# Seven block products for eight in the up projection of a two-layer trunk: what it does on one Trainium2 core

## The chip, the core and the metric

The kernel runs on one core of a Trainium2 chip. The metric is the time of one execution on the device, in microseconds (us); lower is better. The core has a matrix engine (TensorE, PE), VectorE (DVE), ScalarE (ACT), GpSimd (POOL) and SyncE (SP), which issues the DMAs here. The engines run side by side and wait for one another through semaphores.

## The reference

One step of a two-layer trunk over 576 tokens: 64 new tokens of 8 sequences and a prompt of 512. Each layer has a token mixing (attention and two linear recurrences), then a ConvFFN; the change is in the ConvFFN. With D = 1024, D_FF = 2816 and `L` tokens of a sequence:

```python
xn = rms_norm(x, p['g_pre_ffn'])
u = xn @ p['w_up']                                   # (1024) x (1024 x 5632)
ext = jnp.concatenate([conv_prev.astype(u.dtype), u], axis=1)
c = sum(ext[:, j:j + L] * p['w_conv'][j] for j in range(CONV_WIDTH))   # width 3
a, b = jnp.split(c, 2, axis=-1)
ffn = (jax.nn.gelu(a, approximate=True) * b) @ p['w_down']             # (2816 x 1024)
x = x + rms_norm(ffn, p['g_post_ffn'])
```

## The kernel before, in words

Activations lie transposed: features on the 128 partitions (eight k-tiles of the model width, `KT`), the 576 tokens along the free axis, in two halves of 320 and 256 (`HALVES`). Every f32 product is made from two parts of each operand: a high part (a rounded copy) and the low rest. Three matmuls, high x high, high x low, low x high, go into one PSUM bank (`gemm`, L121 to L127).

A weight tile is 128 x 1024. `load_w` (L110) loads it by SP into a raw buffer of a ring of three (`wraw`); `split_w` (L103) has ACT copy the high part `whi` (L106) and DVE subtract for the low part `wlo` (L107).

`ffn` is the loop of interest. The up projection has 44 column tiles a layer, in 22 pairs: tile 2j gives the gelu side of 128 hidden columns, 2j+1 the other. Per up tile (`col_tile`), half 0 is `col_half` (8 x 3 matmuls of 320), half 1 is `joint_half`: `wh` goes against high and low tokens side by side (512 wide, L151), `wl` against the high ones (256 wide, L150 and L153), and ACT's copy (L156) and a DVE add (L157) join the two sums. The first three tiles of a layer are made in `first_tiles`, k-tile by k-tile, as the normed activations come. The evacuation multiplies by the norm's factor `R` into `u` (L1065, L1067, L1069), `conv_end` makes the width-3 convolution (ACT L1083, DVE L1084 and L1085, and two small POOL copies of state, L1076 and L1077), and after the second tile of a pair `h_tile` makes gelu (ACT L1095), the product (DVE L1096) and its split into high and low parts (ACT L1111, DVE L1115).

The down projection is spread over three groups of hidden tiles, and the last five go through `final_phase`, which also makes the closing norm:

```python
FF_GROUPS = ((0, 6), (6, 6), (12, 5))
```

All eight down tiles of a group stand together, behind the up pair after the group's last one (loop at L1143 to L1160). A down tile loads its weights, makes both halves and adds the result to `y` (ACT L1134 in the first group, DVE L1136 and L1139).

On every engine the instructions stand in one order, fixed when the program is built: a scheduler takes them from the order of the code and its costs, `behind(...)` and `manual_schedule` set the rest by hand. An engine that waits holds all that stands behind in its order.

Of the kernel before, what the change touches and what calls it, by code (L numbers as in the profile page):

```python
# [72 lines left out]
def trunk_kernel(ctx: ExitStack, tc: tile.TileContext, I, O):  # L73
# [68 lines left out]
    def joint_half(w, xh, xm, ks, evac, add=None):  # L142


        t0, n = HALVES[1]
        b = main_bank()
        for i, k in enumerate(ks):
            wh, wl = wtile(w, i)
            if i:
                PE.matmul(b[:, :n], wl, xh[k][1], start=False, stop=False)  # L150
            PE.matmul(b[:, :2 * n], wh, xm[k], start=(i == 0), stop=(i == len(ks) - 1))  # L151
            if i == 0:
                PE.matmul(b[:, :n], wl, xh[k][1], start=False, stop=False)  # L153
        if add is None:
            low = columns(n, "low", 2)
            S.activation(low, b[:, n:2 * n], AF.Copy)  # L156
            V.tensor_tensor(b[:, :n], b[:, :n], low, ALU.add)  # L157
        evac(b, 1, t0, n)
        if add is not None:
            add(b[:, n:2 * n], t0, n)  # L160

    def col_tile(w, xh, xl, ks, evac, name=None, xm=None, add=None):
        for hf in range(2):
            with behind(placed.get(FILL.get(f"{name}:{hf}"))):
                if hf and xm is not None:
                    joint_half(w, xh, xm, ks, evac, add)
                else:
                    col_half(w, xh, xl, ks, hf, evac)
# [1203 lines left out]
```

## Time and profile before

| | |
|---|---|
| median of 3 runs | 1708.03 us (1703.61 to 1710.71) |
| profiled execution | 1708.13 us, span of its trace 1706.3 us |
| mean granted TensorE clock | 0.989 |

The span runs from the first to the last instruction of the trace; the execution's own time is 1.8 us longer. Rows of groups give line, engine, operation, output <- inputs, tile size and count, then busy time and mean ns of one, and the idle time before them with what ended it. In a timeline, the first number is the start in us from the span's start, the second how long it took; "x3" means that three are shown as one, and a bracket tells an idle time before and its releaser. Layer 0's up tiles begin at 447 us.

### The profile page before, as it was taken

What the parts mean: (1) busy time and instruction counts of PE and PEld (TensorE: products, weight loads), DVE (VectorE), ACT (ScalarE), POOL (GpSimd) and SP (SyncE); (2) the same over time, 40 slices, a digit from 0 to 9 for tenths busy, and PEclk for the clock granted to TensorE, in tenths of its full rate; (3) what the DMA queues carried; (4) which work ended last, traced back from release to release, by engine and by line L of the source; (5) the groups of instructions that cost most, each with busy time, mean ns of one, the idle gap of its engine ahead of it and who ended that gap; (6) DMA issues with size and microseconds to landing.
All of it is one profiled execution on the core that took longest, in us unless ns stands there. A gap on an engine that the chain in (4) does not pass through costs nothing.

```text
span 1706.3 us, 34557 instructions
## 1 busy us (share of the span) xinstructions
PE 1655.1 (97%) x13840; PEld 1541.0 (90%) x13840; DVE 1118.3 (66%) x2270; ACT 780.4 (46%) x1376; POOL 525.6 (31%) x800
## 2 busy tenths in 40 slices
PE   8999999999999999999989999989999999999997
PEld 8888997789899999999988899968998999999997
DVE  6765756557774674776657657566578737757764
ACT  6744425574543442443456544255645434324431
POOL 4554332304420220230365453332053202103203
PEclk9999999999999999999999999999999999999999
DMA  5221336846344535633222212378555355266231
GB/s 184 70 70 58 103 116 241 335 169 258 136 148 161 198 107 215 230 120 112 97 79 83 76 64 79 120 299 312 186 201 185 109 195 206 73 234 255 70 105 56
DMA packets 65664, 260.83 MB, mean 153 GB/s; under 512 B 9664, under 2 KB 18144, under 8 KB 63968
## 3 DMA queue, kind: packets, MB, share of 16 engines
q1 hardware_dynamic: 65504, 258.62, 43.1%
q8 instruction: 109, 1.79, 0.4%
q14 instruction: 51, 0.42, 0.1%
HBM read 245.39 MB, written 80.31 MB: 191 GB/s over the span
## 4 chain that ended last, share of the span: by engine, by line
PE 86%; ACT 4%; POOL 3%; DVE 3%; issue 2%; DMA 1%; SPq 0%; POOLq 0%; ACTq 0%; DVEq 0%
PE ps_m L125 18%; PE ps_m L127 18%; PE ps_m L126 18%; PE ps_m L151 12%; PE ps_m L150 5%; PE ps_s L511 2%; PE ps_o L983 1%; PE ps_o L887 1%; PE ps_s L897 1%; POOL x L370 1%; PE ps_m L663 1%; PE ps_t L916 1%; PE ps_m L153 1%; PE ps_m L421 1%; PE ps_s L949 1%
## 5 line engine op out<-in xcount | busy, mean ns | idle before, releaser
L125 PE MATMUL ps_m<-xha,whi 128*128 128x320 f32 x1088 | 342.2, 315 | 3.1 <-ACT whi L106 2.6
L126 PE MATMUL ps_m<-xla,whi 128*128 128x320 f32 x1088 | 341.3, 314 | 0.0
L127 PE MATMUL ps_m<-xha,wlo 128*128 128x320 f32 x1088 | 340.2, 314 | 0.9 <-DVE wlo L107 0.9
L107 DVE TENSOR_TENSOR wlo<-wraw,whi 128x1024 fp32r<-128x1024 f32 (+4 forms) x232 | 259.0, 1121 | 77.2 <-ACT whi L106 74.9
L106 ACT ACTIVATE whi<-wraw 128x1024 fp32r<-128x1024 f32 (+4 forms) x232 | 221.1, 959 | 169.4 <-PE ps_m L126 64.7
L151 PE MATMUL ps_m<-xm,whi 128*128 128x512 f32 x656 | 237.6, 396 | 0.0
L126 PEld LDWEIGHTS ps_m<-xla,whi 128*128 128x128 f32 x1088 | 207.0, 190 | 5.8 <-issue 2.0
L125 PEld LDWEIGHTS ps_m<-xha,whi 128*128 128x128 f32 x1088 | 207.2, 190 | 5.5 <-ACT whi L106 2.8
L127 PEld LDWEIGHTS ps_m<-xha,wlo 128*128 128x128 f32 x1088 | 206.7, 190 | 3.1 <-issue 1.4
L150 PE MATMUL ps_m<-xm,wlo 128*128 128x256 f32 x574 | 161.2, 281 | 0.0
L125 PE MATMUL ps_m<-hh,whi 128*128 128x320 f32 (+1 forms) x512 | 154.1, 301 | 0.0
L126 PE MATMUL ps_m<-hh,whi 128*128 128x320 f32 (+1 forms) x512 | 154.1, 301 | 0.0
L127 PE MATMUL ps_m<-hh,wlo 128*128 128x320 f32 (+1 forms) x512 | 154.0, 301 | 0.0
L1077 POOL COPY cso<-u 128x2 f32<-128x2 f32 x88 | 79.2, 900 | 209.9 <-DVE u L1069 209.4
L151 PEld LDWEIGHTS ps_m<-xm,whi 128*128 128x128 f32 x656 | 123.3, 188 | 22.4
L127 PE MATMUL ps_m<-xm,wlo 128*128 128x256 f32 x432 | 124.6, 288 | 0.0
L125 PE MATMUL ps_m<-xm,whi 128*128 128x256 f32 x432 | 124.5, 288 | 0.0
L126 PE MATMUL ps_m<-xm,whi 128*128 128x256 f32 x432 | 123.5, 286 | 0.0
L150 PEld LDWEIGHTS ps_m<-xm,wlo 128*128 128x128 f32 x574 | 108.6, 189 | 3.4
L126 PEld LDWEIGHTS ps_m<-hh,whi 128*128 128x128 f32 x512 | 96.5, 188 | 1.5
L125 PEld LDWEIGHTS ps_m<-hh,whi 128*128 128x128 f32 x512 | 96.5, 189 | 0.3 <-DVE y L400 0.3
L127 PEld LDWEIGHTS ps_m<-hh,wlo 128*128 128x128 f32 x512 | 96.7, 189 | 0.0
(326 smaller groups left out, 3843.6 us busy)
## 6 DMA issues: line engine op xcount, KB each, us to landing
wraw<-in_w_up SPq DMA_DIRECT2D x88, 512.0 KB, 3.6
kv<-in_ck SPq DMA_DIRECT2D x32, 768.0 KB, 6.9
kv<-in_cv SPq DMA_DIRECT2D x32, 768.0 KB, 6.9
out_ck<-in_ck SPq DMA_DIRECT2D x32, 768.0 KB, 7.5
out_cv<-in_cv SPq DMA_DIRECT2D x32, 768.0 KB, 6.7
wraw<-in_w_s SPq DMA_DIRECT2D x42, 512.0 KB, 3.7
wraw<-in_w_dn SPq DMA_DIRECT2D x32, 384.0 KB, 3.1
wraw<-in_w_v SPq DMA_DIRECT2D x12, 512.0 KB, 3.6
```

Source lines behind the costliest of these rows:

```text
L106: S.activation(hi[:, :n], raw[:, :n], AF.Copy)
L107: V.tensor_tensor(lo[:, :n], raw[:, :n], hi[:, :n].bitcast(F32), ALU.subtract)
L125: PE.matmul(out, ah, bh, start=(i == 0), stop=False)
L126: PE.matmul(out, ah, bl, start=False, stop=False)
L127: PE.matmul(out, al, bh, start=False, stop=(i == n - 1))
L150: PE.matmul(b[:, :n], wl, xh[k][1], start=False, stop=False)
L151: PE.matmul(b[:, :2 * n], wh, xm[k], start=(i == 0), stop=(i == len(ks) - 1))
L153: PE.matmul(b[:, :n], wl, xh[k][1], start=False, stop=False)
L370: (V if dram_out and k % 4 == 3 else G).tensor_tensor(xk, xk, yk, ALU.add)
L421: PE.matmul(b[:, :n], wh, xh, start=(k == 0), stop=False)
L511: mm = PE.matmul(bp[64 * hh:64 * hh + 64, cp * nh * 32:(cp + 1) * nh * 32], xk[:, c0:c0 + 64], moving(c0), start=True, stop=True)
L1077: G.tensor_copy(cso[:, ui, 16:18], u[:, NU - 2:NU])
```

## The change

Pairs 4 to 21 of each layer ("fast pairs") are made by Strassen's scheme: the 1024 model features are taken as two halves, the pair's two column tiles as two, the 576 tokens as two halves of 288. Eight block products become seven (`products`), each of 4 k-tiles x 3 matmuls x 288 columns, that add up in three banks; ACT keeps copies of partial sums (`keep`), and VectorE or ACT evacuates the sums into `u`.

Both operands need sums of blocks. For the tokens `combine` makes them once a layer, in four parts behind up tiles 3 to 6: it scales by the gain and `R` first (so the fast evacuation has no factor), builds sums in `y` (not yet in use) and splits seven blocks into high and low parts. For the weights `weights` makes four block adds of 512 columns on DVE for each pair and splits 3 x 1024 + 512 columns, instead of 2 x 1024.

Pairs 0 to 3 stay plain, with the joint half replaced by 8 x 3 matmuls of 256 there and in all down tiles. The down tiles form four groups and stand one, two or four at a time behind single pairs (`FF_AFTER`). The convolution's `c` has two buffers instead of three, and hidden tiles 2 to 9 of the ring of ten lie where the activations lay. `x` is written out to DRAM at the end of each mixing (16 stores of half a tile) and read back (8 loads) before `final_phase`, since its place is used for the new weight tiles.

```diff
-FF_GROUPS = ((0, 6), (6, 6), (12, 5))
+FF_GROUPS = ((0, 4), (4, 4), (8, 4), (12, 5))
+FF_AFTER = ({4: 2, 5: 2, 6: 2, 7: 2}, {8: 2, 9: 2, 10: 2, 11: 2}, {12: 2, 13: 2, 14: 2, 15: 2},
+            {17: 1, 18: 1, 19: 1, 20: 1, 22: 4})
...
+            def combine(i):
+                with behind(last_lo[0].ins):
+                    x1, x2, ua, ta = (y[4 * (i % 2) + m] for m in range(4))
+                    for k, d in ((i, x1), (i + HK, x2)):
+                        V.scalar_tensor_tensor(d, xt[k], gnorm(l, 2, k), R, ALU.mult, ALU.mult)
+                    V.tensor_tensor(ua[:, :SH], x1[:, :SH], x1[:, SH:], ALU.subtract)
+                    V.scalar_tensor_tensor(ua[:, SH:], x2[:, SH:], -1.0, ua[:, :SH], ALU.mult, ALU.subtract)
+                    V.tensor_tensor(ta[:, :SH], x2[:, SH:], x1[:, SH:], ALU.subtract)
+                    V.scalar_tensor_tensor(ta[:, SH:], ua[:, SH:], -1.0, x2[:, :SH], ALU.mult, ALU.subtract)
+                    hi, lo = (cp.tile([P, 7 * SH], F32R, name=f"{n}{i}", tag=f"{n}{i}") for n in ("sxh", "sxl"))
+                    for src, m, n in ((x1[:, :SH], B11, 1), (x2, B21, 2), (ua, U1, 2), (ta, T3, 2)):
+                        cols = slice(m * SH, (m + n) * SH)
+                        S.activation(hi[:, cols], src, AF.Copy)
+                        V.tensor_tensor(lo[:, cols], src, hi[:, cols].bitcast(F32), ALU.subtract)
...
+            def weights(j):
+                r0, r1 = (wp.tile([P, WN], F32, name="wraw", tag="wraw", bufs=3) for _ in range(2))
...
+                w0 = split_w(r0, WN, sw, 2)
+                V.tensor_tensor(ws[:, b], r0[:, a], r1[:, a], ALU.add)
+                V.tensor_tensor(r1[:, a], r1[:, a], r1[:, b], ALU.add)
+                V.tensor_tensor(ws[:, a], r0[:, a], r1[:, a], ALU.add)
+                w2 = split_w(ws, WN)
+                w1 = split_w(r1, WN, sw, 2)
+                V.tensor_tensor(r0[:, b], r0[:, b], ws[:, a], ALU.add)
+                w3 = split_w(r0[:, b], HW)
...
+                product(ba, w0, 0, B11)
+                p1 = keep(ba)
+                product(bb, w0, 1, B21)
+                e1(0, lambda d, c: V.tensor_tensor(d, c(bb), c(p1), ALU.add))
+                product(ba, w2, 0, U2, True)
+                p16 = keep(ba)
+                product(bc, w1, 0, U1)
+                p5 = keep(bc)
+                product(ba, w2, 1, T3, True)
+                e2(1, lambda d, c: V.scalar_tensor_tensor(d, c(ba), -1.0, c(p5), ALU.mult, ALU.subtract))
+                product(bc, w3, 0, B22, True)
+                e1(1, lambda d, c: V.tensor_tensor(d, c(bc), c(p16), ALU.add), True)
+                product(ba, w1, 1, T4, True)
+                e2(0, lambda d, c: S.activation(d, c(ba), AF.Copy, scale=-1.0), True)
```

Three places of the program's order show what moves. In each row stands the line, the operation, output <- inputs with buffer numbers, and the size. The first place is VectorE around the evacuation of up tile 6 of layer 0 (`u_5907`; `u_5970` is tile 7's), before:

```order
L1069 TENSOR_TENSOR u_5907<-ps_m_5937,rbc_5168 128x256
L1115 TENSOR_TENSOR hh_5894<-c_5888,hh_5894 128x64
L1115 TENSOR_TENSOR hh_5894<-c_5888,hh_5894 128x2x256
L1065 TENSOR_TENSOR u_5970<-ps_m_5973,rbc_5168 128x8x8
L1067 TENSOR_TENSOR u_5970<-ps_m_5973,rbc_5168 128x256
L1084 SCALAR_TENSOR_TENSOR c_5960<-u_5907,par_90,c_5960 128x592
L1085 SCALAR_TENSOR_TENSOR c_5960<-u_5907,par_90,c_5960 128x592
L157 TENSOR_TENSOR ps_m_6000<-ps_m_6000,low_6017 128x256
L1069 TENSOR_TENSOR u_5970<-ps_m_6000,rbc_5168 128x256
L107 TENSOR_TENSOR wlo_6174<-wraw_6171,whi_6173 128x1024
```

and with the change (tile 6's is `u_5998`; `wlo_6167`, `wlo_6178` and `wlo_6174` are low parts of pair 4's weights, `sxl2` and the rows of L1119 and L1121 are `combine`):

```order
L114 TENSOR_TENSOR wlo_6167<-wraw_6161,whi_6166 128x1024
L1119 SCALAR_TENSOR_TENSOR y6_4689<-y5_4688,y6_4689 128x288
L1121 SCALAR_TENSOR_TENSOR y3_4686<-y2_4685,y1_4684 128x288
L114 TENSOR_TENSOR wlo_6178<-wraw_6162,whi_6177 128x1024
L1126 TENSOR_TENSOR sxl2_5981<-y2_4685,sxh2_5980 128x576
L1077 SCALAR_TENSOR_TENSOR c_5778<-u_5720,par_90,c_5778 128x592
L114 TENSOR_TENSOR wlo_6174<-ws_6165,whi_6173 128x1024
L1055 TENSOR_TENSOR u_5998<-ps_m_6001,rbc_5168 128x8x8
L1055 TENSOR_TENSOR u_5998<-ps_m_6001,rbc_5168 128x256
L1055 TENSOR_TENSOR u_5998<-ps_m_6028,rbc_5168 128x256
L1143 TENSOR_TENSOR wraw_6161<-wraw_6161,ws_6165 128x512
```

The ten rows before hold one weight split of 1024 columns among the evacuations; now three splits, of the next pair, and pieces of `combine` stand ahead of the tile's first evacuation.

The second place is VectorE in the up tiles, before (tiles 10 and 11 of layer 0):

```order
L1069 TENSOR_TENSOR u_6177<-ps_m_6207,rbc_5168 128x256
L107 TENSOR_TENSOR wlo_6372<-wraw_6369,whi_6371 128x1024
L1084 SCALAR_TENSOR_TENSOR c_6230<-u_6177,par_90,c_6230 128x592
L1065 TENSOR_TENSOR u_6240<-ps_m_6243,rbc_5168 128x8x8
L1067 TENSOR_TENSOR u_6240<-ps_m_6243,rbc_5168 128x256
L1085 SCALAR_TENSOR_TENSOR c_6230<-u_6177,par_90,c_6230 128x592
L157 TENSOR_TENSOR ps_m_6270<-ps_m_6270,low_6287 128x256
L1069 TENSOR_TENSOR u_6240<-ps_m_6270,rbc_5168 128x256
L107 TENSOR_TENSOR wlo_6444<-wraw_6441,whi_6443 128x768
```

and in the steady loop of the fast pairs (pair 9: `u_7301` and `u_7304` are its tiles; `wlo_7512`, `wlo_7521` and `wlo_7516` are pair 10's `w2`, `w3` and `w1`; the rows of L1206 evacuate a down tile):

```order
L1180 SCALAR_TENSOR_TENSOR u_7304<-ps_m_7307,acc_7364 128x288
L114 TENSOR_TENSOR wlo_7512<-ws_7503,whi_7511 128x1024
L1182 TENSOR_TENSOR u_7301<-ps_t_7309,acc_7350 128x288
L114 TENSOR_TENSOR wlo_7521<-wraw_7499,whi_7520 128x512
L1206 TENSOR_TENSOR y3_4686<-y3_4686,ps_m_7471 128x320
L1076 SCALAR_TENSOR_TENSOR c_7394<-u_7301,par_90,c_7394 128x592
L1077 SCALAR_TENSOR_TENSOR c_7394<-u_7301,par_90,c_7394 128x592
L1206 TENSOR_TENSOR y3_4686<-y3_4686,ps_m_7485 128x256
L114 TENSOR_TENSOR wlo_7516<-wraw_7500,whi_7515 128x1024
L1076 SCALAR_TENSOR_TENSOR c_7414<-u_7304,par_90,c_7414 128x592
```

The rows before hold a split of 1024 and one of 768; those of the change 1024, 512 and 1024, with both evacuations of a down tile between them, and the low part of `w1` last.

The third place is ScalarE at the same pair 9 (`u_7304` from `ps_m_7307` is the evacuation of its last product T4, `whi_7515` the high part of pair 10's `w1`):

```order
L113 ACTIVATE whi_7511<-ws_7503 128x1024
L113 ACTIVATE whi_7520<-wraw_7499 128x512
L1075 ACTIVATE c_7394<-u_7301,par_90 128x592
L1184 ACTIVATE u_7304<-ps_m_7307 128x8x8
L1184 ACTIVATE u_7304<-ps_m_7307 128x224
L113 ACTIVATE whi_7515<-wraw_7500 128x1024
L1075 ACTIVATE c_7414<-u_7304,par_90 128x592
L1086 ACTIVATE c_7394<-c_7394 128x592
```

The high part of `w1` for the next pair stands directly behind the evacuation of this pair's last product.

## Rows read from the trace of the kernel before

**Rows 1.** The page's engine line and chain: busy us, share of the span, instructions.

```profile
PE 1655.1 (97%) x13840; PEld 1541.0 (90%) x13840; DVE 1118.3 (66%) x2270; ACT 780.4 (46%) x1376; POOL 525.6 (31%) x800
...
PE 86%; ACT 4%; POOL 3%; DVE 3%; issue 2%; DMA 1%; SPq 0%; POOLq 0%; ACTq 0%; DVEq 0%
```

**Rows 2.** Windows: length, busy PE, PEld, DVE, ACT, POOL, granted clock, DMA share, GB/s.

```profile
415.00:447.00 32.00, 28.18 (x210) 27.00 (x208) 25.59 (x52) 16.14 (x35) 23.18 (x34) 0.99 0.06 16
447.00:520.00 73.00, 73.00 (x457) 69.10 (x457) 57.79 (x104) 34.87 (x57) 16.79 (x51) 0.98 0.48 171
520.00:640.00 120.00, 120.00 (x760) 113.15 (x759) 75.26 (x128) 47.80 (x81) 19.44 (x50) 1.00 0.47 162
...
447.00:449.50 2.50, 2.50 (x11) 2.50 (x11) 2.31 (x5) 1.62 (x3) 0.56 (x3) 0.50 0.91 303
449.50:452.00 2.50, 2.50 (x18) 2.50 (x18) 0.41 (x1) 0.91 (x2) 0.00 (x0) 0.96 1.33 539
```

**Rows 3.** PE's timeline in an up tile, then in the final phase.

```profile
504.77 0.31 PE L125 MATMUL ps_m<-xha,whi 128*128 128x320 f32 x1
...
508.29 0.39 PE L151 MATMUL ps_m<-xm,whi 128*128 128x512 f32 x1
...
511.10 0.31 PE L125 MATMUL ps_m<-xha,whi 128*128 128x320 f32 x1
...
795.33 0.30 PE L125 MATMUL ps_m<-hh,whi 128*128 128x320 f32 x1
...
797.53 0.28 PE L125 MATMUL ps_m<-hh,whi 128*128 128x256 f32 x1
...
799.30 0.31 PE L125 MATMUL ps_m<-hh,whi 128*128 128x320 f32 x1
```

**Rows 4.** PE's timeline behind a wait, at the start of layer 0's up tiles.

```profile
446.18 1.16 PE L292 MATMUL ps_t<-con,rr 128*128 128x128 f32 x4 [1.33 <-POOL rr L266]
447.00 0.61 PE L125 MATMUL ps_m<-xha,whi 128*128 128x320 f32 x1
...
449.54 0.38 PE L125 MATMUL ps_m<-xha,whi 128*128 128x320 f32 x1
449.76 0.30 PE L126 MATMUL ps_m<-xla,whi 128*128 128x320 f32 x1
```

**Rows 5.** VectorE's timeline in layer 0's first up tiles.

```profile
444.33 3.50 DVE L107 TENSOR_TENSOR wlo<-wraw,whi 128x1024 fp32r<-128x1024 f32 x3
447.80 0.76 DVE L1069 TENSOR_TENSOR u<-ps_s,rbc 128x256 f32<-128x256 f32 x2
...
454.71 0.83 DVE L1085 SCALAR_TENSOR_TENSOR c<-u,par,c 128x592 f32<-128x592 f32 x1
455.46 0.42 DVE L157 TENSOR_TENSOR ps_m<-ps_m,low 128x256 f32<-128x256 f32 x1
455.79 0.82 DVE L1085 SCALAR_TENSOR_TENSOR c<-u,par,c 128x592 f32<-128x592 f32 x1
```

**Rows 6.** VectorE's groups by form, whole span.

```profile
L107 DVE TENSOR_TENSOR wlo<-wraw,whi 128x1024 fp32r<-128x1024 f32 x162 | 201.5, 1247 | 59.8 <-ACT whi L106 57.8
L1084 DVE SCALAR_TENSOR_TENSOR c<-u,par,c 128x592 f32<-128x592 f32 x88 | 73.0, 829 | 2.9 <-ACT c L1083 2.6
```

**Rows 7.** ScalarE's groups by form, whole span.

```profile
L106 ACT ACTIVATE whi<-wraw 128x1024 fp32r<-128x1024 f32 x162 | 170.3, 1054 | 108.2 <-PE ps_m L126 44.3 <-PE ps_m L151 22.5 <-DMA wraw<-in_w_dnf 11.6
L1083 ACT ACTIVATE c<-u,par 128x592 f32<-128x592 f32 x88 | 69.2, 790 | 33.5 <-DVE u L1069 31.5
L156 ACT ACTIVATE low<-ps_m 128x256 f32<-128x256 f32 x82 | 31.0, 378 | 75.9 <-PE ps_m L151 75.9
```

**Rows 8.** Loads of up weights issued from 640 to 760 us: issue to landing.

```profile
DMA to landing us min/median/max: 3.1/3.5/5.3
```

**Rows 9.** GpSimd's groups by form, whole span.

```profile
L1077 POOL COPY cso<-u 128x2 f32<-128x2 f32 x88 | 79.2, 900 | 209.9 <-DVE u L1069 209.4
...
L1076 POOL COPY cso<-u 128x16 f32<-128x16 f32 x88 | 18.5, 213 | 234.7 <-DVE u L1065 234.4
```

More of the change, by code (lines that the diff above doesn't have):

```diff
@@ L140, in col_half, with col_tile @@
         evac(b, hf, t0, n)
[L142 to L162, printed above, removed]
+    def col_tile(w, xh, xl, ks, evac, name=None):
         for hf in range(2):
             with behind(placed.get(FILL.get(f"{name}:{hf}"))):
[L165 to L168, printed above, removed]
+                col_half(w, xh, xl, ks, hf, evac)
     placed = {}
@@ new lines, in fast_pair, with products, product, keep @@
+            def fast_pair(j):
+                with behind(last_lo[0].ins if j == NPLAIN else None):
+                    w0, w1, w2, w3 = weights(j)
+                e1, e2 = (conv_begin(2 * j + i)[1] for i in range(2))
+                with behind(last_mm[0].ins if j == NPLAIN else None):
+                    products(w0, w1, w2, w3, e1, e2)
+            def products(w0, w1, w2, w3, e1, e2):
+                def product(b, w, half, m, more=False):
+                    cols = slice(m * SH, (m + 1) * SH)
+                    for i in range(HK):
+                        wh, wl = wtile(w, half * HK + i)
+                        xh, xl = (v[:, cols] for v in xs[i])
+                        PE.matmul(b, wh, xh, start=i == 0 and not more, stop=False, skip_group_check=more)
+                        PE.matmul(b, wl, xh, start=False, stop=False, skip_group_check=more)
+                        PE.matmul(b, wh, xl, start=False, stop=i == HK - 1, skip_group_check=more)
+                def keep(b):
+                    d = columns(SH, "acc", 3)
+                    S.activation(d, b, AF.Copy)
+                    return d
+                ba, bb, bc = (b[:, :SH] for b in (main_bank(), s_bank(), t_bank()))
+                product(ba, w0, 0, B11)
[12 more added lines that the diff above has]
+                e2(0, lambda d, c: S.activation(d, c(ba), AF.Copy, scale=-1.0), True)
@@ L1157, in ffn @@
                 ws = [load_w(I["w_dnf"][l, i], pool=wf, bufs=FIN) for i in range(FIN)]
+                for k in range(KT):
+                    xt[k] = xpool.tile([P, T], F32, name=f"x{k}")
+                    with behind(last_w[0].ins):
+                        SP.dma_start(xt[k], xdr[:, k, :])
                 nxt = None if last else [load_w(I["w_s"][l + 1, i]) for i in range(NFIRST)]
```

145 lines of the change are left out of this document (79 added, 66 removed).

## The prediction

> **What bounds the kernel now.** I read the page's engine line and chain first: PE is busy 97% of the span and carries 86% of the chain that ended last; DVE is next with 66% [rows 1]. The table by stage shows where those shares differ [rows 2]. From 447 us on, in the up tiles of layer 0, PE is busy 73.00 of 73 us, then 120.00 of 120, and DVE 57.79 of 73 (79%) in the first stretch, 63% in the next; in 415 to 447, where the mixing ends, DVE is at 80% and PE waits 3.8 us. So PE alone sets the time of the up and down tiles, and VectorE has least to spare exactly where the new `combine` is put.
>
> Is PE limited by columns or by matmuls? In PE's own timeline [rows 3] the half tile from 504.77 to 508.29 is 24 matmuls of 320 columns: 146.7 ns from start to start. In the final phase 15 of 320 take 2.20 us and 15 of 256 take 1.77 us, 118 ns each. Both are 0.459 ns a column, with 2 ns left over per matmul. The joint half, 512 and 256 wide, takes 2.81 us for 8 x 768 columns, 0.457 ns a column: the same price. A whole up tile is 6.33 us (504.77 to 511.10). Only after a wait is it dearer: after PE's 1.33 us without work before 446.18 its matmuls stand 265 ns apart until 449.54, and 140 to 147 ns again from there [rows 4]. The clock granted from 447.00 to 449.50 is 0.50, the level of 1.2 GHz, and 0.96 in the 2.5 us behind [rows 2]; the ten matmuls to 449.76 take 2.76 us instead of 1.47, a loss of 1.3.
>
> **What the fast pairs take from PE.** Two old up tiles are 2 x 8 x 3 x 576 = 27,648 columns; seven products of 4 blocks x 3 matmuls x 288 are 24,192. The 3,456 that go are worth 3,456 x 0.4585 ns = 1.585 us a pair, and 36 pairs (18 in each layer) make **-57.0 us**. The four more matmuls of a pair cost 4 x 2 ns, nothing. Plain up tiles and down tiles that lose their joint half keep 768 columns a k-tile, at the same price: 0.
>
> These rows speak on width from 256 to 512, and 288 lies between, so this term has narrow ends. A rule of the Trainium skill (page "TensorE: Matmul & The Clock Gate", section "Back-to-back issue gap") would leave almost nothing of it: in a stream of loads and matmuls both set the spacing, it says, with 81 ns for 128 columns and 131 ns for 512. A straight line between these gives an estimate of 102 ns for 288 and 106 for 320, and a pair would gain about 0.2 us instead of 1.6. The trace disagrees: its joint half needs 2.81 us for 16 matmuls, about 234 ns for one of 512 and 118 for one of 256. It decides.
>
> **What VectorE gets.** Prices from start to start [rows 5]: 1.157 us for 1024 columns (three in 3.47 us), 0.33 for 256; a line through both gives 0.61 for 512, 0.68 for 576, 0.365 for 288. The three-operand form takes 0.75 for 592, so 0.73 for 576 and 0.43 for 288. In a steady fast pair VectorE does 3 x 1.157 + 0.61 (four splits) + 4 x 0.61 (block adds) + 1.25 (four evacuations of halves, less the one that is ACT's) + 4 x 0.75 (convolution) + 0.69 + 0.8 (the product and its split) = 12.3 us; a down tile of four k-tiles adds 0.61 + 0.40 + 0.33 = 1.3. PE needs 7 x 1.585 = 11.1 a pair and 4 x 3 x 576 x 0.4585 = 3.17 a down tile of four k-tiles. So:
> - pairs 4 to 15, two down tiles each: PE 17.4, VectorE 15.0 (86%);
> - pairs 17 to 20, one each (of five k-tiles): PE 15.1, VectorE 13.8;
> - pairs 16 and 21, none: PE 11.1, VectorE 12.3, late by 1.2.
>
> **The head of each FFN.** VectorE works in written order, and `combine` plus the first `weights` come before anything can start on pair 4. From the first plain split (444.33 in [rows 5]) to the low part of the second fast pair's `w1`, VectorE's new order holds 113 instructions: 11 of 1024 columns (12.7 us), 11 of 512 (6.7), 20 of 576 (8.2 + 5.8), 20 of 592 (12.0 + 2.8), 22 of 288 (4.7 + 3.9), 20 of 224 or 256 (6.6) and 9 of 64 (1.3): 64.7 us without a single wait, to 509.0. PE's work to the product that needs it: it starts at 447.0, +1.3 for the half clock, five plain tiles of 6.33, seven products of pair 4 and the first of pair 5 at 1.585, and 3.7 of down tiles: 496.3. PE is 12.7 us late there. Wherever VectorE is the last it also waits: for ACT (which has to make each high part first, 1.05 us [rows 7]), and for tiles to evacuate. The first place shown of the order has such a case: tile 6's first half, of which VectorE frees the bank, now stands behind three weight splits of 1024 of pair 4; tile 7's halves are queued behind that bank on PE. And PE pays half clock after each longer wait, as in [rows 4]. The floor is 12.7 if all waits lie beside one another; the ceiling is the low parts' mean duration of 1.247 us in place of 1.157 and 0.829 for 0.75 [rows 6], some 2 us, and on top a wait for ACT's high part at ten of the 1024-wide pieces, 1.05 each. I take 15 for a layer, near the floor since ACT has half its time free in 447 to 520 (34.87 of 73 [rows 2]): **+30** (25 to 50).
>
> **The steady loop.** After a pair's last product (T4) ACT evacuates it (about 0.5 us, between the 256-column copy's 0.378 and the 592-column pass's 0.790 [rows 7]), then makes the high part of the next `w1`, 1.05, and VectorE its low part, 1.16; the third place shown has this order. The next pair's U1 needs both, and only P1 and a down half lie before it on PE: 1.585 + about 1.4 = 3.0 us. That is 2.7 plus semaphores: an even race. The low part also frees a raw buffer for the next load, which lands 3.5 us later (3.1 to 5.3 [rows 8]), is split in 2.2, and is wanted by U2's product 7.9 us into the period: freed about 1.4 us into it, 1.4 + 5.7 = 7.1 plus queues leaves little to spare. Down weights take buffers from the same ring of three. Nothing in before's trace shows this loop; its least is nothing, its most one DMA landing too late each pair, 1.8 us (5.3 - 3.5). I take 0.5 us a pair in the 14 pairs that run into it, nearer the least because the rows' medians fit: **+7** (0 to 65). Pairs 16 to 21 add 2 x 1.2 a layer, less what the neighbours lend: **+4** (0 to 8).
>
> The stores of x at the mixing's end, 16 a layer, and eight loads before the final phase cost nothing: SP's queue has room (DMA share 6% in 415 to 447 [rows 2]), and the final phase's first 11 us of matmuls hide the loads. Without that cover it is one landing, 5 us a layer. Fewer conv buffers (two for three) hold only where `c` is late: part of the loop's term. Four down groups for three mean 8 more down tiles a layer with two evacuations each, 0.73 us of VectorE, counted in the periods above; in return the joint half's ACT copy (0.378 [rows 7]) and VectorE add go, a third of a us each at each of 82 tiles. PE is alone in the stretches where they stood, so they free nothing.
>
> **Sum:** -57 + 30 + 7 + 4 = -16. The profiled execution took 1708.13 us (span 1706.3, 1.8 around it), 0.1 above the median of 1708.03, so 1692.
>
> **The rivals.** A measurement of this kernel tells about 0.5%, 8.5 us, from no change.
> - *VectorE keeps up* (16%). If the head's waits lie beside PE's work (PE starts pair 4 late but catches up within pairs where VectorE has 14% to spare, since a late PE only moves), 10 a layer go and the loop costs nothing: below 1676, at best 1651. Against it: the head's 12.7 is counted without waits.
> - *The head costs twice* (22%): 1699.5 to 1716.6. Splits held by GpSimd would do it: its two-column copy takes 900 ns where the sixteen-column one takes 213 [rows 9], so something holds these two apart; if VectorE were held as long, 0.7 us for eight copies in a head, +6 a layer. For VectorE's side the rows show little: 1.247 on average against 1.16 alone. The Trainium skill (page "SBUF — State Buffer", section "🔬 SBUF: two separate sides") says that the two engines share a port pair that one holds for a whole instruction, when VectorE reads two operands from SBUF; the new block adds do that. The 900 ns agree.
> - *The loop overruns its period* (20%, slower). T4, ACT's evacuation, the split, U1, then the raw buffer's load: if the chain is longer than 17.4 us, PE waits in every pair and gets half clock after it. Without the loop's own 7 and 4 the sum is 1681; each us of overrun costs 36. It decides from 0.75 us a pair (1708); at 1.5 us, two half-clock restarts or a down load in front of the raw one, 1735. For it: two engines hand over four times in 3 us. Against: PE has the down tiles to fill with, and they lie in written order between the products.
> - *Narrow matmuls cost as much as wide ones* (2%): no -57, then 1749. The 118 ns for 256 columns speak against it.
>
> **Chances and range.** My forecast (1676 to 1699.5) has 40%. Faster is that and full gain, 0.56; same 0.22; slower 0.22. The range goes from 1660 (leaving about a third of the full-gain case) to 1726 (leaving the worse half of the overrun): about 0.18 outside. Its own range for the likeliest is 1676 to 1700.
>
> **What would show it.** Right: start-to-start 132 ns for 288 columns, 1.59 us a product; in 447 to 520 DVE above 95% and PE below 85%, waiting for `wlo` and for banks; from pair 5 on PE 97% or more with waits under 0.5 us before U1. Wrong: waits of over 1 us at the same product of every pair (the overrun), or PE full through the head. A total outside 1660 to 1726 makes a term wrong.

## The result, and the profile after

The changed kernel takes 1683.21 us, the median of 4 runs (1681.14 to 1685.94), against 1707.03 us for the kernel before on the same chip (4 runs): ratio 0.9861, 95% interval 0.9835 to 0.9887, 23.8 us less. The prediction was 1692, in a range of 1660 to 1726. Faster was right, and the time lies in the span that the prediction called likeliest (1676 to 1699.5); the gain is half again as large as the 16 us that were forecast. The profiled execution took 1681.14 us, with a span of 1679.4.

The page of the changed kernel, its engine line and its chain, against [rows 1]:

```profile
PE 1606.9 (96%) x14256; PEld 1526.1 (91%) x14256; DVE 1248.1 (74%) x2472; ACT 877.6 (52%) x1638; POOL 556.9 (33%) x800
...
PE 76%; DVE 10%; ACT 5%; POOL 3%; issue 3%; DMA 2%; POOLq 0%; SPq 0%; ACTq 0%; DVEq 0%
```

VectorE has 130 us more work, as it should, and it is now on the path that sets the end: 10% of the chain instead of 3%. PE is busy 48 us less, and 21 us of that come back as idle time (51 us of the span before, 72 now). Where? The windows of the changed kernel, with the columns of [rows 2]:

```profile
447.00:475.00 28.00, 27.66 (x206) 27.43 (x205) 28.00 (x56) 16.27 (x26) 9.29 (x13) 1.00 0.52 187
475.00:485.00 10.00, 0.42 (x4) 0.19 (x2) 10.00 (x17) 3.66 (x6) 5.30 (x5) 0.68 0.09 26
485.00:507.00 22.00, 21.43 (x149) 21.20 (x149) 21.84 (x40) 13.52 (x28) 11.45 (x15) 0.91 0.36 133
507.00:520.00 13.00, 12.93 (x97) 12.49 (x96) 10.75 (x20) 8.61 (x20) 1.41 (x5) 1.00 0.63 218
520.00:700.00 180.00, 179.98 (x1355) 179.60 (x1354) 152.84 (x257) 96.11 (x183) 30.75 (x82) 1.00 0.52 182
700.00:760.00 60.00, 59.28 (x443) 58.59 (x443) 53.97 (x92) 33.39 (x63) 15.23 (x32) 1.00 0.52 190
```

Up to 507 us VectorE is without a gap (59.84 of 60 us); PE stands still for nearly all of the ten microseconds from 475. From 520 to 700, the steady fast pairs, PE is busy 179.98 of 180 us, with VectorE at 85%. So the loss is in the head, as the prediction had it, and the steady loop costs next to nothing.

What PE waits for, from its timeline: the end of the long wait, the last of the slow matmuls behind it, and one product of a fast pair.

```profile
484.95 0.55 PE L132 MATMUL ps_m<-xm,whi 128*128 128x256 f32 x1 [9.58 <-DVE u L1055]
...
488.72 0.31 PE L134 MATMUL ps_m<-xm,wlo 128*128 128x256 f32 x1
...
491.17 0.29 PE L1162 MATMUL ps_s<-sxh,whi 128*128 128x288 f32 x1
...
492.76 0.30 PE L1162 MATMUL ps_t<-sxh,whi 128*128 128x288 f32 x1
```

Tile 7's second half (it reads `xm`) needs the bank that VectorE frees with tile 6's evacuation (L1055). VectorE's own timeline just ahead shows it on its way there, step by step through the order quoted above (the first place): three weight splits and pieces of `combine`, with no idle time in any row. It then goes on without a wait to the split that ends the 113 instructions:

```profile
478.70 1.21 DVE L114 TENSOR_TENSOR wlo<-wraw,whi 128x1024 fp32r<-128x1024 f32 x1
...
480.58 1.22 DVE L114 TENSOR_TENSOR wlo<-wraw,whi 128x1024 fp32r<-128x1024 f32 x1
...
483.13 1.22 DVE L114 TENSOR_TENSOR wlo<-ws,whi 128x1024 fp32r<-128x1024 f32 x1
484.26 0.88 DVE L1055 TENSOR_TENSOR u<-ps_m,rbc 128x64 f32<-128x64 f32 x3
...
506.35 1.23 DVE L114 TENSOR_TENSOR wlo<-wraw,whi 128x1024 fp32r<-128x1024 f32 x1 [0.16 <-ACT whi L113]
```

That last split starts at 506.35 and ends about 1.16 later, 507.5. The prediction had counted 64.7 us from the first split; it began at 443.67 here, so 508.4.

For the experiments one measure is better than the whole time, since the mixings differ by some us from run to run: the stretch from the start of the up tiles (PE's broadcast of `rr`) to the closing norm (its broadcast of `rp`), the "FFN stretch" below. In PE's timeline of the changed kernel its ends are

```profile
445.51 0.71 PE L276 MATMUL ps_t<-con,rr 128*128 128x128 f32 x4 [1.32 <-POOL rr L250]
...
846.88 0.38 PE L276 MATMUL ps_t<-con,rp 128*128 128x128 f32 x2
...
1276.64 0.60 PE L276 MATMUL ps_t<-con,rr 128*128 128x128 f32 x3 [1.32 <-POOL rr L250]
...
1670.86 0.71 PE L276 MATMUL ps_t<-con,rp 128*128 128x128 f32 x4 [1.04 <-POOL rp L250]
```

so 401.4 us in layer 0 and 394.2 in layer 1. Before it was 413.9 (446.18 in [rows 4] to 860.06) and 405.6 (1292.19 to 1697.79): 12.5 and 11.4 less. The two make 23.9 us, as much as the whole time fell, so the mixings, with their stores of `x`, got no longer.

One part of this measure does not come from the edits. Behind the wait of 1.3 us at its start, PE's first 10 to 14 matmuls of 320 columns stand some 265 ns apart in some of the profiled executions, as in [rows 4], and 147 in others, which makes 1.3 to 1.6 us. Before has this half-clock start in both layers, the change only in layer 1:

```profile
445.98 0.39 PE L132 MATMUL ps_m<-xha,whi 128*128 128x320 f32 x1
446.21 0.31 PE L133 MATMUL ps_m<-xla,whi 128*128 128x320 f32 x1
446.35 0.31 PE L134 MATMUL ps_m<-xha,wlo 128*128 128x320 f32 x1
...
1277.39 0.47 PE L133 MATMUL ps_m<-xla,whi 128*128 128x320 f32 x1
1277.65 0.47 PE L134 MATMUL ps_m<-xha,wlo 128*128 128x320 f32 x1
```

In a kernel where PE waits for VectorE in the head, a half-clock start only makes that wait shorter (in the change 8.61 us in layer 1, 0.34 and 9.58 in layer 0). Where PE never waits, as before and with all tiles plain, it counts in full.

### The profile page after: what moved, and what is told of

The parts are those of the page before. It is cut to its first block, busy times and chain, and to the rows that moved or that the text cites. A ratio compares the mean times of both kernels' runs of the same rounds, so it can differ in the third digit from the quotient of the medians.

```text
span 1679.4 us, 35933 instructions
## 1 busy us (share of the span) xinstructions
PE 1606.9 (96%) x14256; PEld 1526.1 (91%) x14256; DVE 1248.1 (74%) x2472; ACT 877.6 (52%) x1638; POOL 556.9 (33%) x800
## 4 chain that ended last, share of the span: by engine, by line
PE 76%; DVE 10%; ACT 5%; POOL 3%; issue 3%; DMA 2%; POOLq 0%; SPq 0%; ACTq 0%; DVEq 0%
PE ps_m L132 14%; PE ps_m L134 13%; PE ps_m L133 13%; PE ps_m L1164 4%; PE ps_m L1162 4%; PE ps_m L1163 4%; DVE wlo L114 2%; PE ps_t L1163 2%; PE ps_t L1164 2%; PE ps_t L1162 2%; PE ps_s L493 2%; DMA wraw<-in_w_up 1%; PE ps_o L965 1%; PE ps_o L869 1%; POOL x L352 1%
## 5 line engine op out<-in xcount | busy, mean ns | idle before, releaser
L133 PE MATMUL ps_m<-xla,whi 128*128 128x320 f32 x864 | 270.9, 314 | 0.0
L134 PE MATMUL ps_m<-xha,wlo 128*128 128x320 f32 x864 | 268.4, 314 | 0.5 <-DVE wlo L114 0.5
L132 PE MATMUL ps_m<-xm,whi 128*128 128x256 f32 x864 | 248.6, 288 | 18.5 <-DVE u L1055 18.5
L133 PE MATMUL ps_m<-xm,whi 128*128 128x256 f32 x864 | 246.9, 286 | 0.0
L132 PEld LDWEIGHTS ps_m<-xm,whi 128*128 128x128 f32 x864 | 165.9, 192 | 22.0 <-issue 20.5
L1162 PE MATMUL ps_m<-sxh,whi 128*128 128x288 f32 x576 | 170.0, 296 | 0.7 <-ACT acc L1168 0.7
L1163 PE MATMUL ps_m<-sxh,wlo 128*128 128x288 f32 x576 | 169.7, 295 | 0.0
L1164 PE MATMUL ps_m<-sxl,whi 128*128 128x288 f32 x576 | 169.7, 295 | 0.0
L133 PEld LDWEIGHTS ps_m<-xm,whi 128*128 128x128 f32 x864 | 166.1, 192 | 1.5 <-issue 1.1
L1162 PEld LDWEIGHTS ps_m<-sxh,whi 128*128 128x128 f32 x576 | 108.4, 188 | 1.2 <-ACT acc L1168 1.2
L1163 PEld LDWEIGHTS ps_m<-sxh,wlo 128*128 128x128 f32 x576 | 108.7, 189 | 0.0
L1164 PEld LDWEIGHTS ps_m<-sxl,whi 128*128 128x128 f32 x576 | 108.3, 188 | 0.0
```

The source lines that it names most:

```text
L134: last_mm[0] = PE.matmul(out, al, bh, start=False, stop=(i == n - 1))
L1162: PE.matmul(b, wh, xh, start=i == 0 and not more, stop=False, skip_group_check=more)
L1163: PE.matmul(b, wl, xh, start=False, stop=False, skip_group_check=more)
L1164: PE.matmul(b, wh, xl, start=False, stop=i == HK - 1, skip_group_check=more)
```

## The experiments

**Theory 1**: VectorE's sum of work in the head, which comes in one written order, makes PE late; the order only chooses where the lateness shows. **Rivals**: the order itself costs (PE waits for a bank that VectorE could have freed); GpSimd and VectorE hold one another; the loop from T4 to the next pair's U1 costs. Every time has its ratio to the kernel before on its own chip. FFN stretches, in us:

| kernel | layer 0 | layer 1 | median, ratio to before (95%) |
|---|---|---|---|
| before | 413.9 | 405.6 | |
| the change | 401.4 | 394.2 | 1683.2, 0.9861 (0.9835 to 0.9887) |
| all tiles plain | 415.1 | 407.1 | 1712.1, 1.0014 (1.0000 to 1.0028) |
| evacuation first | 403.9 | 395.3 | 1690.4, 0.9875 (0.9848 to 0.9902) |
| no low parts, GpSimd writes zeros | 397.5 | 391.2 | 1679.3, 0.9818 (0.9792 to 0.9844) |
| no low parts, ACT writes zeros | 397.0 | 390.0 | 1674.5, 0.9813 (0.9794 to 0.9831) |
| no combine, late copies | 391.6 | 385.8 | 1669.6, 0.9787 (0.9773 to 0.9802) |
| low parts on GpSimd | 406.2 | 398.4 | 1693.1, 0.9921 (0.9891 to 0.9950) |
| sixteen pieces on GpSimd, evacuation first | 408.3 | 401.5 | 1699.0, 0.9955 (0.9938 to 0.9972) |
| 5 plain pairs | 400.5 | 394.0 | 1685.1, 0.9872 (0.9849 to 0.9894) |
| 3 plain pairs | 406.8 | 396.9 | 1692.0, 0.9924 (0.9904 to 0.9944) |
| down tiles together | 419.3 | 412.5 | 1721.9, 1.0070 (1.0046 to 1.0094) |
| slow loop | 412.4 | 405.8 | 1706.9, 1.0003 (0.9992 to 1.0013) |

### Is the gain the products' alone?

```diff
-NEX = 2
-NPLAIN = 4
-COMBINE = (3, 4, 5, 6)
+NEX = 10
+NPLAIN = 22
+COMBINE = ()
```

> All 44 up tiles plain (no combine, no fast pairs); the four down groups, their spreading, the x round trip and the halves without joint sums stay as in the change. Theory 1 (the gain is the products' alone): the columns on PE are those of the kernel before, so 1706 to 1713 us, ratio to before 1.000 to 1.004. Rival (the spread down tiles and the lost ACT and VectorE adds of the joint halves bring part of the gain): 1690 to 1702 us.

Theory 1 holds: 1.0014, and the FFN stretch is 1.2 and 1.5 us longer than before. Before has the half-clock start in both layers (1.3 and 1.6 us) and this run in neither, so like for like it is 2.5 and 3.1 us longer. The halves of 256 that took the joint half's place in every up and down tile that had one cost at most that; the spread down tiles alone give nothing.

### Order or work?

```diff
+                    def put(d, c):
+                        ev = V.tensor_tensor(d, c(b), c(r), ALU.mult)
+                        if ui == 6:
+                            last_ev[0] = ev
+                    place(t0, n, put)
...
-                with behind(last_lo[0].ins if j == NPLAIN else None):
+                with behind(last_ev[0].ins if j == NPLAIN else None):
```

> One condition changed: pair 4's weight splits are put behind up tile 6's evacuation instead of ahead of it; same instructions, other order on VectorE. Theory 1 (VectorE's sum of work, 65 us in one row, makes PE late in the head, wherever the lateness shows): the wait of 9.6 and 8.6 us on tile 6's bank goes, and waits of nearly the same sum come at pair 4's and 5's weights: 1677 to 1687 us. Rival (the order itself costs: PE stands still for a bank that VectorE could have freed): both waits and the half clock after them go, 2 x 11 us: 1659 to 1667 us.

The ratio is the change's within its interval (the time of 1690.4 us lies 3 above Theory 1's range), and the FFN stretch is 2.5 and 1.1 us longer, not 11 shorter. PE's waits in this kernel, in sum, times and longest:

```profile
PE ps_m L132 <- DVE u L1056: 6.6, 3, 3.6
...
PE ps_t L1167 <- DVE wlo L114: 4.6, 4, 1.4
PE ps_m L132 <- ACT xha L1101: 4.1, 2, 2.0
```

The 18.5 us on tile 6's bank fell to 6.6, and waits for low parts of weights and for hidden tiles came in their place: PE's waits in the head sum to 8.9 us in layer 0 and 9.9 in layer 1, against 10.5 and 9.2 in the change. VectorE again stands idle for less than 1 us up to 507. The order chose the place of the wait; it did not make it.

### Less work on VectorE

```diff
-                        V.tensor_tensor(lo[:, cols], src, hi[:, cols].bitcast(F32), ALU.subtract)
+                        if m in (U1, T3):
+                            G.memset(lo[:, cols].bitcast(F32), 0.0)
+                        else:
+                            V.tensor_tensor(lo[:, cols], src, hi[:, cols].bitcast(F32), ALU.subtract)
```

> Leaves out the low parts of the four summed token blocks (U1, U2, T3, T4): GpSimd writes zeros in their place, so VectorE has 8 instructions of 576 columns fewer in each head, 8 x 0.68 = 5.4 us; the output is less exact. Theory 1 (VectorE's work in the head): PE is earlier by 5.4 us a layer, 10.9 us in all, and its half clock stays: 1669 to 1676 us. Rival (the wait is one of order or of a buffer, and VectorE would be in time without it): 1681 to 1685 us. Second rival (GpSimd's writes hold VectorE through a shared port): gain under 5 us.

3.9 and 3.0 us less in the FFN stretches, 56 to 72% of what Theory 1 asked (5.4). The second rival is not tested by this run: GpSimd's writes wait for nothing, so all of them lie ahead of the FFN stretch. In layer 0 five of the eight stand here, the other three 4 us earlier:

```profile
426.29 2.66 POOL L1127 MEMSET sxl<- 128x576 f32 x5
```

In a second run ACT wrote the zeros:

```diff
-                            G.memset(lo[:, cols].bitcast(F32), 0.0)
+                            S.activation(lo[:, cols], src, AF.Copy, scale=0.0)
```

> As the run without the low parts of the four summed token blocks, but ACT writes the zeros instead of GpSimd; the output is less exact. Theory 1 with a port shared by GpSimd and VectorE (GpSimd's eight writes took a part of the gain back): 4.9 to 5.4 us a layer less than the change from the start of the up tiles to the closing norm, 396 to 397 and 389 to 390 us, in all 1671 to 1676 us. Rival (only a part of what VectorE saves reaches PE, whoever writes the zeros): 3 to 4 us a layer, as with GpSimd, in all 1676 to 1680 us.

4.4 and 4.3 us: between the two, 80% of what VectorE saves. The wait on tile 6's bank is 5.6 us in each layer instead of 9.6 and 8.6. The 0.5 and 1.3 us between the two runs can't be GpSimd's writes in the head, where there are none, and their cause is open, as is about 1 us a layer to 5.4. By their ratios the two runs are as fast as one another, and the fastest of the study with the products of the change, but by a less exact result; no kernel with the full result beat the change.

Then all of `combine`'s arithmetic was left out.

```diff
-                    x1, x2, ua, ta = (y[4 * (i % 2) + m] for m in range(4))
-                    for k, d in ((i, x1), (i + HK, x2)):
-                        V.scalar_tensor_tensor(d, xt[k], gnorm(l, 2, k), R, ALU.mult, ALU.mult)
-                    V.tensor_tensor(ua[:, :SH], x1[:, :SH], x1[:, SH:], ALU.subtract)
...
+                    x1, x2 = xt[i], xt[i + HK]
+                    ua, ta = x1, x2
...
-                        V.tensor_tensor(lo[:, cols], src, hi[:, cols].bitcast(F32), ALU.subtract)
+                        S.activation(lo[:, cols], src, AF.Copy, scale=2.0 ** -12)
```

> Leaves out combine's arithmetic on VectorE (the scaling by gain and R, the sums, the low-part subtractions: 36 instructions, 21.8 us a layer by the start-to-start prices); ACT copies raw blocks of x into the high and the low tiles instead, so PE, DMAs and all that follows stay the same and the up projection of the fast pairs is of other numbers. Theory 1 (VectorE's work in the head is the whole price of the head): the long waits vanish, the stretch from the start of the up tiles to the closing norm gets 11 to 13 us shorter in each layer, 1657 to 1663 us, ratio 0.970 to 0.974. Rival (half of the head's price is the start of the loop, the first loads and splits of weights): 1668 to 1676 us.

Measured: 1679.8 us, 0.9845 (0.9821 to 0.9868). This run tells less than it should. ACT's copies need only `x`, so they went ahead of the mixing's closing norm, and the up tiles began at 462.97 instead of 445.51; the FFN stretches of 384.6 and 377.7 leave out work that was done earlier. It was repeated with copies of `R`, which is there only at the start of the up tiles:

```diff
-                    x1, x2 = xt[i], xt[i + HK]
-                    ua, ta = x1, x2
+                    x1 = x2 = ua = ta = R
```

> As the run without combine's arithmetic, but ACT fills the blocks with copies of R, which is there only when the up tiles begin, so that no copy can go ahead of the mixing's closing norm (in the run before they did, and held the start of the up tiles back). The up projection of the fast pairs is of other numbers. Read by the stretch from the start of the up tiles (PE's broadcast of rr) to the closing norm (its broadcast of rp): in the change 401.4 us in layer 0 and 394.2 in layer 1. Theory 1 (VectorE's work in the head is its whole price): 388 to 391 and 381 to 384 us, in all 1657 to 1664 us. Rival (half of the price is the start of the loop, the first loads and splits): 394 to 398 and 387 to 391, in all 1668 to 1676 us.

9.7 and 8.4 us less, between the two; the whole time of 1669.6 lies in the rival's range, but the up tiles of layer 0 begin 2.8 us later than the change's, since copies of the first half of `R` still go ahead. Why not 12? PE's and VectorE's timelines in its layer 0:

```profile
479.98 0.55 PE L132 MATMUL ps_m<-xm,whi 128*128 128x256 f32 x1 [6.14 <-DVE u L1055]
```

```profile
467.02 0.77 DVE L1087 TENSOR_TENSOR c<-c 128x592 f32<-128x592 f32 x1 [2.64 <-ACT c L1086]
468.54 1.22 DVE L114 TENSOR_TENSOR wlo<-wraw,whi 128x1024 fp32r<-128x1024 f32 x1 [0.75 <-ACT whi L113]
```

PE still waits for the same bank, but now VectorE has idle time ahead of it: it waits for ACT's gelu, which stands behind 23 of this experiment's copies of 576 columns. So `combine`'s arithmetic is worth at least 8.4 us a layer; what the head would cost without ACT's copies stays open. Here, with VectorE no longer full, the order may well be what holds PE; evacuating first together with less work was not tried.

### Can GpSimd take a part?

```diff
-                        V.tensor_tensor(lo[:, cols], src, hi[:, cols].bitcast(F32), ALU.subtract)
+                        (G if m in (U1, T3) else V).tensor_tensor(lo[:, cols], src, hi[:, cols].bitcast(F32), ALU.subtract)
```

> The eight low-part subtractions of 576 columns for the summed token blocks go from VectorE to GpSimd; everything else as in the change, result complete. Theory 1 (VectorE's work sets the head): as without them, 5.4 us a layer less on VectorE, ratio to before 0.979 to 0.983, the two long waits on tile 6's bank 4 to 6 us each. Rival (GpSimd and VectorE hold one another when both read two operands): VectorE's instructions in the head grow longer than in the change (512-wide adds above 0.75 us, 592-wide ones above 0.95), the gain is under 3 us: 0.984 to 0.990.

The rival's mechanism, and dearer than it said: 4.9 and 4.2 us more. VectorE's groups by form in 447 to 510 us, of the change and then of this kernel:

```profile
L1077 DVE SCALAR_TENSOR_TENSOR c<-u,par,c 128x592 f32<-128x592 f32 x9 | 7.4, 826 | 0.0
L1087 DVE TENSOR_TENSOR c<-c 128x592 f32<-128x592 f32 x4 | 3.1, 764 | 0.0
L1118 DVE TENSOR_TENSOR y<-y 128x288 f32<-128x288 f32 x4 | 1.8, 445 | 0.0
L1138 DVE TENSOR_TENSOR ws<-wraw 128x512 f32<-128x512 f32 x2 | 1.4, 682 | 0.0
```

```profile
L1077 DVE SCALAR_TENSOR_TENSOR c<-u,par,c 128x592 f32<-128x592 f32 x8 | 7.8, 973 | 0.0
L1087 DVE TENSOR_TENSOR c<-c 128x592 f32<-128x592 f32 x4 | 4.3, 1074 | 0.0
L1118 DVE TENSOR_TENSOR y<-y 128x288 f32<-128x288 f32 x4 | 3.0, 756 | 0.0
L1138 DVE TENSOR_TENSOR ws<-wraw 128x512 f32<-128x512 f32 x2 | 2.2, 1084 | 0.5 <-DMA wraw<-in_w_up 0.5
```

The means of these kinds are 0.15 to 0.4 us longer, though nothing of them was changed, and other kinds are as long as in the change. Behind each raised mean stands a single long instruction that begins while one of GpSimd's 576-wide subtractions (2.02 us on average) runs. One such pair, GpSimd's instruction and then VectorE's, which takes 0.45 us alone:

```profile
469.83 1.66 POOL L1126 TENSOR_TENSOR sxl<-y,sxh 128x576 fp32r<-128x576 f32 x1
```

```profile
470.12 1.68 DVE L1118 TENSOR_TENSOR y<-y 128x288 f32<-128x288 f32 x1
```

In layer 0 there are eight of them, one for each subtraction, 0.8 to 1.2 us longer each and 9.3 in all. VectorE gave away 5.4 us and got 9.3 back. With twice as many pieces moved it gets worse:

```diff
-                    V.tensor_tensor(ua[:, :SH], x1[:, :SH], x1[:, SH:], ALU.subtract)
+                    G.tensor_tensor(ua[:, :SH], x1[:, :SH], x1[:, SH:], ALU.subtract)
...
-                    V.tensor_tensor(ta[:, :SH], x2[:, SH:], x1[:, SH:], ALU.subtract)
+                    G.tensor_tensor(ta[:, :SH], x2[:, SH:], x1[:, SH:], ALU.subtract)
```

> Both: the eight subtractions of 576 and the eight of 288 columns of the token sums on GpSimd, and pair 4's weight splits behind tile 6's evacuation. VectorE has 8 x 0.68 + 8 x 0.365 = 8.4 us less in each head. Theory 1: PE's lateness in the head falls from about 12 to about 4 us a layer: ratio to before 0.975 to 0.979. Rival (GpSimd at 1.7 us for a 576-wide piece becomes the late one: its chain of sums ends after VectorE's did): 0.984 or more, PE waits for token blocks.

0.9955, and 7.0 and 7.2 us more than the change: Theory 1 with its 8.4 us falls for this kernel, since the work that it moved was not free. PE does not wait for token blocks, so it is not GpSimd that is late; VectorE's 1024-wide splits take 1.53 us in this head instead of 1.22.

### More or less plain work in front

```diff
-NPLAIN = 4
-COMBINE = (3, 4, 5, 6)
+NPLAIN = 5
+COMBINE = (3, 4, 6, 8)
...
-FF_AFTER = ({4: 2, 5: 2, 6: 2, 7: 2}, {8: 2, 9: 2, 10: 2, 11: 2}, {12: 2, 13: 2, 14: 2, 15: 2},
+FF_AFTER = ({5: 2, 6: 3, 7: 3}, {8: 2, 9: 2, 10: 2, 11: 2}, {12: 2, 13: 2, 14: 2, 15: 2},
```

> One more plain pair (5 plain, 17 fast a layer; token sums behind tiles 3, 4, 6 and 8; first down group behind pairs 5, 6, 7 with 2, 3, 3). PE gets 1.53 us more work a layer and VectorE a tile pair of slack (12.7 us of PE for 8.8 of VectorE) before the first fast pair. Theory 1: lateness falls by 3.9 a layer and 1.5 come back, so 2.4 us a layer less than the change: 1677 to 1684 us. Rival (the lateness is not VectorE's work: hidden tile 2 waits for the last plain tile's activations and holds the convolution's two buffers): 1686 to 1695 us.

0.9 and 0.2 us less in the FFN stretches, and the same time as the change within the intervals: neither theory's number. The wait is one, 7.7 us in each layer (9.6 and 8.6 in the change), and with the shorter wait about as much is won as the missing fast pair costs. With a plain pair fewer (`NPLAIN = 3`, `COMBINE = (3, 4, 5, 5)`):

> One plain pair fewer (3 plain, 19 fast a layer; token sums behind tiles 3, 4 and twice 5; down tiles as in the change). PE gets 1.53 us less work a layer, VectorE loses a pair of plain tiles as cover (3.9 us). Theory 1: 2.4 us a layer more than the change, 1685 to 1692 us. Rival (the wait does not depend on how much plain work lies in front): the product's gain counts alone, 3 us less than the change, 1678 to 1682 us.

5.4 and 2.6 us more: Theory 1's side, above its 2.4. PE's timeline in layer 0, where the waits now lie at pair 3's weights:

```profile
473.66 0.61 PE L1162 MATMUL ps_m<-sxh,whi 128*128 128x288 f32 x1 [7.45 <-ACT whi L113]
...
478.40 0.61 PE L1163 MATMUL ps_m<-sxh,wlo 128*128 128x288 f32 x1 [3.19 <-DVE wlo L114]
```

Of the three tried, four plain pairs, or five, are the best place.

### What the spread down tiles and the loop's slack are worth

```diff
-FF_AFTER = ({4: 2, 5: 2, 6: 2, 7: 2}, {8: 2, 9: 2, 10: 2, 11: 2}, {12: 2, 13: 2, 14: 2, 15: 2},
-            {17: 1, 18: 1, 19: 1, 20: 1, 22: 4})
+FF_AFTER = ({4: 8}, {8: 8}, {12: 8}, {17: 8})
```

> The eight down tiles of a group together behind one pair (4, 8, 12, 17), as the kernel before has them; all else as in the change. Theory 1: a fast pair without down tiles needs 12.3 us of VectorE against 11.1 us of PE, so 14 pairs a layer are late by up to 1.2 us each instead of 2 (and half clock after each wait), less what VectorE makes up during the eight down tiles: 1696 to 1712 us. Rival (PE alone sets the steady time, so where the down tiles stand is free): 1681 to 1686 us.

Theory 1's direction and more than its number: 17.9 and 18.3 us more, slower than the kernel before. Only a third of that is the loss that Theory 1 priced. At the same count of columns done by PE, this kernel is 5.7 us behind the change (5.3 in layer 1) near the end of pair 20, and 12 to 13 us come after that, 10 of them in the closing stage. PE's timeline in layer 0 shows two kinds of wait, short ones in the fast pairs that have no down tiles, and a long one at the start of the closing stage. There ACT makes the high parts of its first weights only behind the last hidden tile (at 818.2), and no down tile is left to cover that:

```profile
558.49 0.40 PE L1161 MATMUL ps_m<-sxh,whi 128*128 128x288 f32 x1 [0.55 <-ACT whi L112]
559.47 0.40 PE L1161 MATMUL ps_m<-sxh,whi 128*128 128x288 f32 x1 [0.45 <-ACT acc L1167]
...
819.28 0.63 PE L131 MATMUL ps_m<-xha,whi 128*128 128x320 f32 x1 [5.96 <-ACT whi L112]
```

Layer 1 has the same, with 6.05 at the end.

The loop was tried with a longer path:

```diff
+                for _ in range(3):
+                    last_e2[0] = S.activation(o_bank()[:, :SH], ba, AF.Copy)
                 e2(0, lambda d, c: S.activation(d, c(ba), AF.Copy, scale=-1.0), True)
...
-                w1 = split_w(r1, WN, sw, 2)
+                with behind(last_e2[0].ins if j > NPLAIN else None):
+                    w1 = split_w(r1, WN, sw, 2)
```

> Adds to each fast pair three more ACT copies of T4's sums into an unused bank (3 x 0.38 us) ahead of its evacuation, and puts the next pair's w1 split behind it: the path from T4 to the next U1 gets 1.1 to 2.5 us longer. In the change about 0.5 us lie between the low part of w1 and its first use on PE. Theory 1 (the loop has 0.5 us to spare and no more): 24 pairs with two down tiles lose 0.7 us or more each and pay half clock behind the waits: 1702 to 1735 us, waits in front of U1 in every pair. Rival (other matmuls fill the place, the path decides nothing): 1682 to 1690 us.

The time falls in Theory 1's range, but not in its way. At the same count of columns done by PE, this kernel is about 5 us behind the change after pair 15 and 6.8 after pair 21, in both layers: some 0.4 us a pair, where 0.7 or more was asked. The other 4 to 5 of the 11 us come behind the last pair, in the closing stage. A wait of each place:

```profile
713.64 0.40 PE L1164 MATMUL ps_t<-sxh,whi 128*128 128x288 f32 x1 [1.08 <-ACT whi L113]
...
818.01 0.41 PE L132 MATMUL ps_m<-xha,whi 128*128 128x320 f32 x1 [1.28 <-ACT whi L113]
```

So a us or more on the path is mostly hidden in the pairs. About two fifths of the loss come from the closing stage, where no product is left to hide it.

## Why the prediction was right, and where it was off

**Products (-57.0 predicted).** From 491.17 to 492.76 one product of 12 matmuls takes 1.59 us, 132.5 ns a matmul; 132 were forecast. A pair is 7 x 1.59 = 11.13 us against 12.66, so -1.53 a pair and -55.1 for 36. The halves of 256, which the prediction took as nothing, cost the plain run at most 5.6 us in both layers together, like for like. The change has them in 5 up tiles and in the down tiles' parts from 12 hidden tiles, 136 of the plain run's 424 k-tiles a layer, an estimate of 1.8 us: together -53.3. Matmuls of 288 are priced by column, not by load: the rival of equal prices is out, and with it the estimate from the Trainium skill's "Back-to-back issue gap" (page "TensorE: Matmul & The Clock Gate") of 102 ns for 288 columns and 106 for 320; the trace has 132.5 and 146.7.

**The head (+30, 25 to 50 with its ends).** Right in its mechanism and too dear in its size. VectorE is full, its 113 instructions end within a microsecond of where they were counted to end, and PE is late by a little less than the count said: 12.7 was the floor. In layer 0 the waits are 0.34 + 9.58 + 0.56 = 10.5 us, and 17 matmuls behind the long one (484.95 to 488.72) take 222 ns each instead of 118, 1.8 us more; in layer 1 it is 8.61 + 0.56 and 24 such matmuls, 2.4: 23.9 for both. With the half-clock starts, 2.9 us before and 1.6 in the change, the head costs 22.5 more than before, 11.3 a layer. The step that was mis-sized is "I take 15 for a layer": the waits for ACT that were laid on top of the floor did not come, since ACT's high parts were ready (0.16 us is all VectorE waited before 507). Of its signs, VectorE's (above 95% in 447 to 520) came out with 96.7%, and PE's (below 85%) was just missed with 85.5%. The place was named too, tile 6's bank, but as one case among several; it is nearly the whole wait. That the work and not this place is the cause is shown by the evacuation-first run and by the runs with less work.

**The loop (+7) and the pairs without down tiles (+4).** The loop cost next to nothing from 520 to 700. Its steps run as counted. Rows of PE, then ACT, then VectorE, then PE again, at one end of a pair (`ps_t` at 617.25 is the next U1):

```profile
613.77 0.30 PE L1164 MATMUL ps_m<-sxl,whi 128*128 128x288 f32 x1
...
617.25 0.29 PE L1162 MATMUL ps_t<-sxh,whi 128*128 128x288 f32 x1
```

```profile
614.46 1.06 ACT L113 ACTIVATE whi<-wraw 128x1024 fp32r<-128x1024 f32 x1
```

```profile
615.55 1.23 DVE L114 TENSOR_TENSOR wlo<-wraw,whi 128x1024 fp32r<-128x1024 f32 x1 [0.53 <-ACT whi L113]
```

From T4's last matmul to the low part it takes 3.0 us, and U1 begins 0.5 us after that. The even race is won each time: the scheduler put more of the down tiles' matmuls into the gap than the half tile that the prediction counted. Over the whole, -53.3 + 22.5 = -30.8 leaves 6.9 us to the measured -23.9 in the FFN stretches, for these two terms that were forecast at 11. About 2 of the 6.9 are in waits of 0.25 to 0.5 us that the timeline names; the rest is spread and was not traced.

**The rivals.** Full gain had 16%: the head's 24 us were indeed there. The overrun (20%) did not happen: even with 1.1 us or more added to the loop a pair loses some 0.4 us, not the 0.75 from which this rival decides, though with the closing stage's share the whole gain is gone. The doubled head through GpSimd (22%) did not happen either: the change leaves GpSimd its small copies, and VectorE's 592-wide instructions take 0.826 us in the head, 0.829 before [rows 6]. The run that moved subtractions there shows that this mechanism is real. In that the prediction's view that "for VectorE's side the rows show little" held only as long as GpSimd's instructions were small.

## What to carry to other kernels

Counting the instructions of the second-busiest engine up to the point where the first one needs the result, in its written order and at start-to-start prices, gave the size of the loss within 1.5 us a layer; waits of a third engine, half idle here, did not come on top. A scheme that trades matmuls for additions gains only as long as other matmuls cover its additions: here the same seven products are 1.4% faster with down tiles spread between the pairs and 0.7% slower than the old kernel with them together. A third of that difference is lost in the pairs that have no cover, the larger part behind them, mostly because nothing covers the closing stage's first weights. When one engine is full, look whether the engine that could take its work shares a path with it before moving any.

## What the runs showed of the hardware

GpSimd and VectorE hold one another. GpSimd's sixteen-column copy at the start of a tile, in the group of the changed kernel from 447 to 510 us,

```profile
L1041 POOL COPY u<-cso 128x16 f32<-128x16 f32 x8 | 12.3, 1534 | 15.0 <-DVE c L1077 15.0
```

took 1.53 us on average, against 0.506 in the same stretch of the kernel before:

```profile
L1059 POOL COPY u<-cso 128x16 f32<-128x16 f32 x12 | 6.1, 506 | 18.3 <-DVE c L1085 13.8 <-ACT low L156 2.7 <-DVE u L1065 1.9
```

With eight subtractions of 576 columns moved to GpSimd, eight of VectorE's instructions took 0.8 to 1.2 us longer, one of 288 columns 1.68 us instead of 0.45. The Trainium skill says (page "SBUF — State Buffer", section "🔬 SBUF: two separate sides") that the two share a port pair which one of them has for a whole instruction, on VectorE's side when it reads two operands from SBUF and GpSimd reads there too; the eight long instructions agree.

After a long wait PE's matmuls ran at a granted clock of 0.50, the level of 1.2 GHz: 17 of them behind 9.58 us without work in layer 0, 24 behind 8.61 us in layer 1. So the longer wait was not followed by the longer slow stretch. Behind the wait of 1.32 us at the start of the change's up tiles, 13 matmuls ran at that level in layer 1 and none in layer 0.
